# Forgetting attention: biases carried in the free rows of the second score product, causal mask added on VectorE

## The chip, the cores and the metric

The kernel runs on one core of one Trainium2 chip. The metric is the device time of one execution in microseconds; a profiled execution gives a trace besides, whose span runs from the first to the last instruction. The engines are named as in the profile: PE is TensorE (PEld its weight loads), DVE is VectorE, ACT is ScalarE, POOL is GpSimd, and SP is the engine that issues most of the DMAs.

## What is computed

One inference step of a two-layer decoder trunk for 512 prompt tokens and 8 x 4 sample tokens. Layer 0 is a state-space / sliding-window hybrid, layer 1 is forgetting attention; each is followed by cross-attention and a feed-forward block. The change is in layer 1 alone. For 16 query heads of 64 in 4 key groups it computes:

```python
q, k, v, fg = split(hp @ w_in_odd)
logf = log_sigmoid(fg + fox_fb)                       # (tokens, 16 heads)
cum  = cumsum(logf, axis=tokens)
s = einsum('qkgd,skd->kgqs', q, k) * 64**-0.5
s = s + (cum[t] - cum[s])                             # the forgetting bias
s = where(key <= query, s, -1e30)                     # causal mask
o = einsum('kgqs,skd->qkgd', softmax(s), v)           # in 128-query blocks
```

The term cum[t] is the same for all keys of a query and falls out of the softmax, so the kernel adds only -cum[s]. The sample tokens attend to 1024 cached tokens each (pages of 128 tokens, fetched by a page table) and to themselves.

## The kernel before

Activations lie transposed, features on partitions, tokens along the free dimension. A weight or activation is split into a high part that TensorE's float32r format holds and a low remainder; a linear layer is three products per 128 features (`acc3`). ACT makes the high part, DVE the low one (L158, L159 for weights).

Layer 1 is `odd`. Value and key projections come first, then the log-sigmoid, the cumulative sums, and the query projection in 8 pieces of 128 outputs (`wd_q`, two chunks of 256 and 288 tokens each, 24 products a chunk). The prompt's attention is `fox_prompt(m, c)`: m is a half of the heads (8 of 16), c a block of 128 queries, which looks at W = 128(c+1) keys. Per head it does, in order:

- four products into one PSUM bank (tag `sc`, two banks): the bias row, spread to all queries by a one-hot column (L1101, operand `oddr`); the mask of the last 128 keys in bf16 (L1102, operand `room`, 128 wide); and the scores in two products, `kh` and `kl`, W wide each (L1104). Query tiles `Q` hold the high part in 64 rows and the low part in the other 64; `kh` holds the high part of the keys in both halves of its rows, `kl` the low part in both;
- DVE: the negated maximum over the keys (L1106, TENSOR_REDUCE); ACT: the exponential from the bank into an SBUF tile `prt`, with its sum (L1110, and the read of ACT's accumulator); DVE: the reciprocal (L1111); POOL: the scaling (L1112);
- c+1 transposes on PE (L137, `room,prt`) and copies to `PT`, by DVE for even heads and ACT for odd ones (L1118).

After 8 heads the products with V follow (`PT,odd`), and DVE copies the result (L1125).

Between the heads other work is interleaved by Python generators: during m = 0 the last four query pieces (one chunk each fourth head); during m = 1 the keys and values of the cross-attention memory of the next block (`memory`, `mem_k`, `mem_v`: products `memh`/`meml` with `wxk` and `wxv` weights, "filler" below), and the sample's attention `fox_sample`, four groups G, each with S and `fox_k` products, a softmax, transposes and `fox_v` products; the table `FOX_AT` says after which heads a piece of it is written. Its pages come by SP: a group's 16 key pages and 16 value pages are issued together. The written order gives priorities only. A list scheduler with its own model of time sets the final order on each engine, and each engine then runs its list in order.

Of the kernel before, what the change touches and what calls it, by code (L numbers as in the profile page):

```python
# [9 lines left out]
F32 = mybir.dt.float32  # L10
# [9 lines left out]
P = 128  # L20
# [18 lines left out]
FOX_AT = (0, 2, 2, 3), (0, 1, 3, 5, 6), (1, 2, 6, 7), (1, 1, 5)  # L39
# [63 lines left out]
class Net:  # L103
# [880 lines left out]
    def odd(self, st, nxt, fill):  # L984
        nc, tc, I, O = self.nc, self.tc, self.I, self.O
        with ExitStack() as es:
# [35 lines left out]
            tr = ev.tile([P, 784], F32R, name="oddr")  # L1022
            ncum, self.fsel, oh16 = tr[:, 0:512], tr[:, 512:768], tr[:, 768:784]
            cw = self.H("cumw")
            strip, cum, ncx = cw[:, 0:896], cw[0:16, 896:1408], cw[0:16, 1408:1920]
            self.after(nc.scalar.dma_start(strip, I["strip"]), self.last)
            self.after(nc.vector.tensor_copy(oh16, self.cst[:, C_OH:C_OH + 16]), self.last)
            ps = self.psum("tp", [P, 512])
            for c in range(4):
                o = 384 - 128 * c  # L1030
                self.mm(ps[0:16], lf[:, c], strip[:, o:o + 512], c == 0, c == 3)
            nc.scalar.activation(cum, ps[0:16], AF.Copy, scale=-1.0)
            self.zero(ncum.bitcast(F32))
            nc.vector.tensor_copy(ncum[0:16], cum)
            nc.vector.tensor_tensor(ncx, cum, ncum[0:16].bitcast(F32), ALU.subtract)
            nc.vector.tensor_copy(ncum[32:48], ncx)
# [3 lines left out]
            with tc.tile_pool(name="fox", bufs=1) as fx:  # L1040
                self.pvs, self.heads = [], 0
                self.qst, self.prt = fx.tile([P, 3072], F32R, name="qst"), fx.tile([P, 3712], F32, name="prt")
                self.qs_at = self.pr_at = 0
                K2 = self.stack_k(kT)
# [3 lines left out]
                m0 = self.mark()  # L1048
                self.banks = ['sc']
                f = self.linear_steps(wq, range(4, 8), KD, xh, xl, qe)  # L1050
                smp = self.fox_sample(q, kTs, Qb, ncs, V, lf, fx, S, sel)
                heads = 0
                for c in range(4):
                    for _ in self.fox_prompt(q, K2, V, ncum, oh16, fx, 0, c):
                        heads += 1
                        if heads % 4 == 0:
                            next(f, None)
                        if heads == 16:
                            next(smp)
                for _ in f:  # L1060
                    pass
                self.banks = ['sc', 'sc', 'tr']
                f = fill()
                next(f)
                heads = 0
                for c in range(4):
                    for _ in self.fox_prompt(q, K2, V, ncum, oh16, fx, 1, c, FOX_AT[c], smp):
                        heads += 1
                        if heads % 4 == 0:
                            next(f, None)  # L1070
# [722 lines left out]
```

## Time and profile before

| | |
|---|---|
| median of 3 runs | 1703.76 us (1699.1 to 1706.17) |
| profiled execution | 1705.22 us, span 1703.5 us |
| mean granted clock of PE | 0.992 |
| PE busy | 1657.2 us (97%) |
| PEld busy | 1529.4 us (90%) |
| DVE busy | 1179.1 us (69%) |
| ACT busy | 772.8 us (45%) |
| POOL busy | 328.2 us (19%) |
| first and last product of the prompt's attention scores | 1012.7 and 1174.9 us from the span's start |

Busy time of PE counts matmuls by modelled ends: consecutive matmuls overlap, so the duration of one (0.27 us and more) is longer than the spacing of their starts. Where a cost of PE is asked, the spacing of starts is read. A line number in a row is that of the code before; helpers such as `mm` (L134) and `tr` (L137) carry the line of all their callers, so rows are told apart by the tiles they name.

### The profile page before, as it was taken

How to read it: one execution, taken by the hardware profiler on the slowest of the kernel's cores; microseconds unless marked ns; L12 is line 12 of the kernel's file. 1: busy time of each engine (PE TensorE's matmuls, PEld its weight loads, DVE VectorE, ACT ScalarE, POOL GpSimd, SP SyncE). 2: the span in 40 equal slices, each digit the busy share in tenths (PEclk: the TensorE clock that was granted, in tenths of full speed). 3: DMA queues.
4: the chain of work that ended last, by engine and by line, in shares of the span. 5: the costliest groups of instructions: out<-in, count | busy, mean ns of one | idle time of the engine just before them, and what ended most of it. 6: DMA issues, size and time to landing. Idle time of an engine off the chain costs nothing.

```text
span 1703.5 us, 32512 instructions
## 1 busy us (share of the span) xinstructions
PE 1657.2 (97%) x12848; PEld 1529.4 (90%) x12848; DVE 1179.1 (69%) x2212; ACT 772.8 (45%) x1599; POOL 328.2 (19%) x508
## 2 busy tenths in 40 slices
PE   7999999998999999999999999999999999999997
PEld 6988799886997999999999987666988999999997
DVE  7666678866866887677766656545577877777663
ACT  5255435344545544444445335445535354444444
POOL 5022312566412310000001203111223100000002
PEclk9999999999999999999999999999999999999999
DMA  5211424136532233222323324455551233233212
GB/s 184 64 53 42 145 79 135 47 110 238 185 111 113 87 106 112 81 99 88 106 75 134 125 66 148 132 148 194 184 189 51 75 112 100 90 103 106 75 66 87
DMA packets 71221, 189.28 MB, mean 111 GB/s; under 512 B 7612, under 2 KB 34012, under 8 KB 63452
## 3 DMA queue, kind: packets, MB, share of 16 engines
q1 hardware_dynamic: 69388, 184.84, 32.6%
q8 instruction: 101, 1.65, 0.4%
q10 hardware_dynamic: 1600, 1.83, 0.4%
q0 software_dynamic: 80, 0.52, 0.1%
q14 instruction: 52, 0.43, 0.1%
HBM read 172.22 MB, written 14.95 MB: 110 GB/s over the span
## 4 chain that ended last, share of the span: by engine, by line
PE 89%; DVE 4%; POOL 2%; DMA 2%; issue 1%; ACT 1%; DVEq 0%; ACTq 0%; POOLq 0%
PE ps L134 64%; PE ps L1512 22%; PE ps L137 3%; POOL room L421 1%; ACT split_t L158 0%; DMA lg<-fox_logf,pg 0%; DVE xs L875 0%; DVE split_t L159 0%; POOL sq L417 0%; DVE split_t L1493 0%; DMA room<-wo_e 0%; DVE xn L1450 0%; DVE meml L248 0%; DMA room<-wfi 0%; DMA o_s_ssm<-hb 0%
## 5 line engine op out<-in xcount | busy, mean ns | idle before, releaser
L134 PE MATMUL ps<-xh,split_t 128*128 128x288 f32 (+1 forms) x2304 | 466.1, 294 | 16.6 <-ACT split_t L158 12.0
L134 PEld LDWEIGHTS ps<-xh,split_t 128*128 128x128 f32 x2304 | 372.0, 191 | 23.8 <-ACT split_t L158 13.2
L1512 PE MATMUL ps<-xf,split_t 128*128 128x272 f32 x2592 | 348.9, 289 | 3.1 <-DVE split_t L1493 2.2
L134 PE MATMUL ps<-xl,split_t 128*128 128x256 f32 (+1 forms) x1152 | 338.7, 295 | 1.2 <-DVE xl L248 1.0
L1512 PEld LDWEIGHTS ps<-xf,split_t 128*128 128x128 f32 x2592 | 335.0, 188 | 4.5 <-DVE split_t L1493 3.1
L257 POOL TENSOR_TENSOR room<-room,sq 128x256 f32<-128x256 f32 (+1 forms) x96 | 86.0, 900 | 773.1 <-ACT sq L256 771.3
L134 PEld LDWEIGHTS ps<-xl,split_t 128*128 128x128 f32 x1152 | 219.2, 190 | 6.6 <-issue 4.1
L158 ACT CAST split_t<-room 128x1024 fp32r<-128x1024 f32 (+1 forms) x128 | 130.3, 1019 | 173.5 <-PE ps L134 122.6
L134 PE MATMUL ps<-hh,fs 128*128 128x256 f32 (+1 forms) x1024 | 206.3, 288 | 0.0
L159 DVE TENSOR_TENSOR split_t<-room,split_t 128x1024 fp32r<-128x1024 f32 (+1 forms) x128 | 155.7, 1219 | 30.6 <-ACT split_t L158 29.9
L134 PEld LDWEIGHTS ps<-hh,fs 128*128 128x128 f32 x1024 | 164.9, 188 | 0.4 <-ACT fs L1556 0.4
L1493 DVE TENSOR_TENSOR split_t<-fr,split_t 128x1024 fp32r<-128x1024 f32 x108 | 131.6, 1220 | 33.9 <-ACT split_t L1492 33.8
L1492 ACT CAST split_t<-fr 128x1024 fp32r<-128x1024 f32 x108 | 113.4, 1052 | 86.5 <-PE ps L1512 54.3
L134 PE MATMUL ps<-hl,fs 128*128 128x256 f32 (+1 forms) x512 | 147.3, 288 | 0.0
L134 PE MATMUL ps<-oh,split_t 128*128 128x288 f32 (+1 forms) x512 | 103.3, 294 | 1.2 <-ACT oh L242 1.2
L134 PEld LDWEIGHTS ps<-hl,fs 128*128 128x128 f32 x512 | 96.4, 188 | 0.0
L134 PEld LDWEIGHTS ps<-oh,split_t 128*128 128x128 f32 x512 | 81.7, 188 | 6.6 <-issue 4.4
L1556 ACT CAST fs<-room 128x512 fp32r<-128x512 f32 x64 | 39.4, 619 | 82.5 <-PE ps L134 67.7
L134 PE MATMUL ps<-ol,split_t 128*128 128x288 f32 (+1 forms) x256 | 76.1, 297 | 0.1
L134 PE MATMUL ps<-hh,split_t 128*128 128x256 f32 (+1 forms) x384 | 73.4, 288 | 0.0
L248 DVE SCALAR_TENSOR_TENSOR xl<-x,room,xh 128x256 fp32r<-128x256 f32 (+1 forms) x96 | 69.7, 755 | 5.3 <-ACT xh L247 5.3
L1569 DVE TENSOR_TENSOR x<-x,ps 128x256 f32<-128x256 f32 (+1 forms) x128 | 54.4, 433 | 27.0 <-PE ps L134 26.7
(417 smaller groups left out, 3132.0 us busy)
## 6 DMA issues: line engine op xcount, KB each, us to landing
fr<-wfi SPq DMA_DIRECT2D x36, 1024.0 KB
room<-wfo SPq DMA_DIRECT2D x64, 256.0 KB
room<-wo_e SPq DMA_DIRECT2D x16, 512.0 KB
xk<-mem_k SPq DMA_DIRECT2D x8, 1024.0 KB
xv<-mem_v SPq DMA_DIRECT2D x8, 1024.0 KB
room<-wfi SPq DMA_DIRECT2D x16, 512.0 KB
fox_k<-fox_k SPq DMA_DIRECT2D x64, 128.0 KB
fox_v<-fox_v SPq DMA_DIRECT2D x64, 128.0 KB
```

What stands on the lines that cost most here:

```text
L134: self.nc.tensor.matmul(out, lhsT, rhs, start=start, stop=stop)
L137: self.nc.tensor.transpose(out, in_, self.ident[0:k, 0:k])
L158: nc.scalar.copy(hi[:, 0:n], raw[:, 0:n])
L159: nc.vector.tensor_tensor(lo[:, 0:n], raw[:, 0:n], hi[:, 0:n].bitcast(F32), ALU.subtract)
L248: return nc.vector.scalar_tensor_tensor(ll, src, g, hh.bitcast(F32), ALU.mult, ALU.subtract)
L257: nc.gpsimd.tensor_tensor(acc, acc, sq[:, 0:N], ALU.add)
L421: nc.gpsimd.tensor_tensor(acc, acc, sq, ALU.add)
L1492: nc.scalar.copy(hi, t)
L1493: nc.vector.tensor_tensor(lo, t, hi.bitcast(F32), ALU.subtract)
L1512: self.nc.tensor.matmul(ps, w[a][:, k], x[:, b, k], start=start and k == 0 and i == 0, stop=k == 3 and i == 2, skip_group_check=True)
L1556: nc.scalar.copy(hi, raw)
L1569: nc.vector.tensor_tensor(x, x, ps, ALU.add)
```

## The change

The queries' low part no longer meets the keys' low part: of the second product's 128 rows, 64 are freed, and they carry the biases. Operand `Q[1]` has the high part of the queries in 64 rows and one-hot columns in the others; `kl` has the low part of the keys and, in the free rows, the cumulative sums of the group's heads (high part in 32 rows, remainder in 32). The bias product and the mask product go. The mask is a 512-wide SBUF tile of 384 zeros and 128 mask columns, added by one DVE operation that reads scores and mask, writes (score + mask) times -1 to `prt`, and keeps the minimum as the exponential's bias; ACT then reads `prt` instead of PSUM. `fox_queries` adds a DVE copy of the high part of the queries. `prt` turns through four slots instead of three. The interleaving is set by `FOX_PLAN` (head number to pieces; q = query chunk, s = sample, m = memory), the sample's first loads are written ahead of the first head, the memory's first piece comes at head 34 instead of ahead of head 33, and a group's value pages are issued after the products of the group before instead of with its key pages.

```diff
-FOX_AT = (0, 2, 2, 3), (0, 1, 3, 5, 6), (1, 2, 6, 7), (1, 1, 5)
+FOX_PLAN = {}
+for _a, _heads in (("q", range(4, 33, 4)), ("s", [33,34,36,38,40,41,43,45,47,49,51,53,55,57,59,61]), ("m", range(34, 64, 4))):
+    for _h in _heads:
+        FOX_PLAN[_h] = FOX_PLAN.get(_h, "") + _a
...
-                self.mm(ps[0:16], lf[:, c], strip[:, o:o + 512], c == 0, c == 3)
+                self.mm(ps, pad[:, c].rearrange("p g x -> p (g x)"), strip[:, o:o + 512], c == 0, c == 3)
+            cr = self.H("cumr", F32R)
+            ncum = cr[:, 0:512], cr[:, 512:1024]
+            nc.scalar.activation(ncum[0], ps, AF.Copy, scale=-1.0)
+            nc.vector.scalar_tensor_tensor(ncum[1], ps, -1.0, ncum[0].bitcast(F32), ALU.mult, ALU.subtract)
...
+    def fox_keys(self, kT, ncum):
...
+            nc.vector.tensor_tensor(kl[a, :, r], src, kh[a, :, r].bitcast(F32), ALU.subtract)
+            for m in range(2):
+                g = 32 * (2 * m + r)
+                nc.scalar.copy(kl[b:b + 32, m, r], ncum[0][g:g + 32].bitcast(F32))
+                nc.vector.tensor_copy(kl[b + 32:b + 64, m, r], ncum[1][g:g + 32].bitcast(F32))
+        for j in range(2):
+            Q = self.qst[:, 2048 + 1024 * j:3072 + 1024 * j].rearrange("p (r i t) -> p r i t", r=2, i=4)
+            for r in range(2):
+                b = 64 - 64 * r
+                d = nc.vector.tensor_copy(Q[b:b + 64, r], self.cst[0:64, C_OH:C_OH + 4].unsqueeze(2).to_broadcast([64, 4, 128]))
...
+    def fox_queries(self, q, m, tok):
...
+            nc.scalar.copy(Q[0][a, r], src)
+            nc.vector.tensor_copy(Q[1][a, r], Q[0][a, r].bitcast(F32))
+            nc.vector.tensor_tensor(Q[0][b, r], src, Q[0][a, r].bitcast(F32), ALU.subtract)
...
-                self.mm(sc[:, 0:W], oh16[:, hd:hd + 1].to_broadcast([P, P]), ncum[:, 0:W], True, False)
-                self.mm(sc[:, W - 128:W], self.identb, self.maskb[:, 128:256], False, False)
                 for z in range(2):
-                    self.mm(sc[:, 0:W], Q[:, r, i], K2[z][:, m, r, 0:W], False, z == 1)
+                    self.mm(sc[:, 0:W], Q[z][:, r, i], K2[z][:, m, r, 0:W], z == 0, z == 1)
...
-                nc.vector.tensor_reduce(nm, sc[:, 0:W], AX.X, ALU.max, negate=True)
-                nc.scalar.activation(pr[:, 0:W], sc[:, 0:W], AF.Exp, bias=nm, accum_out=den)
+                nc.vector.tensor_tensor_reduce(pr[:, 0:W], sc[:, 0:W], mask, -1.0, 1e30, ALU.add, ALU.min, nm)
+                nc.scalar.activation(pr[:, 0:W], pr[:, 0:W], AF.Exp, bias=nm, scale=-1.0, accum_out=den)
```

The programs of before and after have the same PE order up to the cumulative sums, and again from the output projection of layer 1 on; the rows between differ at three places that matter below. In the rows, `split_t` with `xh`/`xl` is the query projection's filler, `oddr` the bias, `room 128x128` the mask, `room,prt` the transposes.

PE, block c = 3 of m = 0, two heads, before:

```order
L137 MATMUL ps_11915<-room,prt 128x128 x4
L134 MATMUL ps_12008<-oddr 128x512
L134 LDWEIGHTS room
L134 MATMUL ps_12008<-room 128x128
L134 MATMUL ps_12008<-kh_10828,qst 128x512
L134 MATMUL ps_12008<-kl_10829,qst 128x512
L137 MATMUL ps_11934<-room,prt 128x128 x4
```

and PE at the same place after:

```order
L140 MATMUL ps_11900<-room,prt 128x128 x4
L137 MATMUL ps_12004<-kh_10826,qst 128x512
L137 MATMUL ps_12004<-kl_10827,qst 128x512
L140 MATMUL ps_11917<-room,prt 128x128 x4
L137 MATMUL ps_12021<-kh_10826,qst 128x512
L137 MATMUL ps_12021<-kl_10827,qst 128x512
```

The bias and mask products are gone, and the transposes that stand between two heads are those of the head four places back instead of three. PE, block c = 2 of m = 0, around its fifth head, before:

```order
L134 MATMUL ps_11791<-oddr 128x384
L134 LDWEIGHTS room
L134 MATMUL ps_11791<-room 128x128
L134 MATMUL ps_11791<-kh_10828,qst 128x384
L134 MATMUL ps_11791<-kl_10829,qst 128x384
L134 MATMUL ps_12084<-xl_10100,split_t 128x288
L134 MATMUL ps_12084<-xh_10099,split_t 128x288 x2
L134 MATMUL ps_11678<-PT_11312,odd 64x512 x3
L137 MATMUL ps_11720<-room,prt 128x128 x3
```

and PE there after, from the second head on:

```order
L137 MATMUL ps_11690<-kh_10826,qst 128x384
L137 MATMUL ps_11690<-kl_10827,qst 128x384
L140 MATMUL ps_11602<-room,prt 128x128 x2
L137 MATMUL ps_11706<-kh_10826,qst 128x384
L137 MATMUL ps_11706<-kl_10827,qst 128x384
L137 MATMUL ps_11722<-kh_10826,qst 128x384
L137 MATMUL ps_11722<-kl_10827,qst 128x384
L140 MATMUL ps_11616<-room,prt 128x128 x2
```

The query projection's products, which stood between the heads down to the eighth head of c = 2, now all stand ahead of its second head; none follows. DVE, block c = 3 of m = 0, before:

```order
L1111 RECIPROCAL ty_12015<-ty_12014 128x1
L1106 TENSOR_REDUCE ty_12032<-ps_12027 128x1
L1118 COPY PT_11901<-ps_12020 128x2x128
L1118 COPY PT_11902<-ps_12020 128x2x128
L1111 RECIPROCAL ty_12034<-ty_12033 128x1
L1106 TENSOR_REDUCE ty_12051<-ps_12046 128x1
```

and DVE there after:

```order
L1137 RECIPROCAL ty_11975<-ty_11974 128x1
L1135 ISA prt,ty_11990<-ps_11987,prt 128x512
L1135 ISA ty_11990 128x1
L1115 CAST qst<-qst 64x512
L1116 TENSOR_TENSOR qst<-q_1101_11132,qst 64x512
L1137 RECIPROCAL ty_11992<-ty_11991 128x1
L1135 ISA prt,ty_12007<-ps_12004,prt 128x512
L1135 ISA ty_12007 128x1
```

The new operation is two DVE instructions, a wide one and one of 128x1; as before, the reciprocal of one head stands ahead of the wide pass of the next.

More of the change, by code (lines that the diff above doesn't have):

```diff
@@ L1218, in fox_sample @@
             if G < 3:
-                kd = load(G + 1, kd)
+                load(keys, G + 1, "fox_k")
             yield
@@ L1248, in fox_sample @@
             self.sample_o(q, Osb, G, 1)
+            if G < 3:
+                load(vals, G + 1, "fox_v")
             yield
```

124 lines of the change are left out of this document (61 added, 63 removed).

## The prediction

> **What bounds the kernel now.** I read the chain of work that ended last first, by engine:
>
> ```profile
> PE 89%; DVE 4%; POOL 2%; DMA 2%; issue 1%; ACT 1%; DVEq 0%; ACTq 0%; POOLq 0%
> ```
>
> PE carries the end nearly everywhere, so a product taken away there is worth its time unless PE then waits. The orders agree outside the stretch from the cumulative sums to the output projection, so I read that stretch by windows (busy us, with counts, of PE, PEld, DVE, ACT, POOL; then PE's clock, DMA share, GB/s):
>
> ```profile
> 980.00:1008.00 28.00, 25.95 (x186) 23.10 (x185) 13.46 (x25) 7.85 (x8) 0.00 (x0) 0.94 0.20 59
> 1008.00:1030.00 22.00, 22.00 (x174) 20.88 (x174) 14.88 (x40) 12.76 (x33) 3.46 (x9) 1.00 0.24 73
> 1050.00:1070.00 20.00, 20.00 (x117) 13.20 (x114) 15.39 (x38) 13.03 (x37) 7.66 (x15) 1.00 0.68 210
> 1070.00:1090.00 20.00, 18.59 (x121) 11.13 (x121) 11.76 (x28) 7.66 (x20) 2.77 (x4) 1.00 0.27 80
> ```
>
> PE is full until 1070, but in 1050 to 1070 DVE is at 15.4 of 20 us: the wide blocks load DVE most. Then I read instructions in order of time. First PE, one head each of c = 3, 2, 1 and 0 (start, us, engine, line, operation):
>
> ```profile
> 1066.98 0.48 PE L134 MATMUL ps<-oddr 128*128 128x512 f32 x1
> 1067.30 0.23 PE L134 MATMUL ps<-room 128*128 128x128 bf16 x1
> 1067.34 0.47 PE L134 MATMUL ps<-kh,qst 128*128 128x512 f32 x1
> 1067.65 0.39 PE L134 MATMUL ps<-kl,qst 128*128 128x512 f32 x1
> 1067.88 0.60 PE L137 MATMUL ps<-room,prt 128*128 128x128 f32 x4
> 1068.24 0.47 PE L134 MATMUL ps<-oddr 128*128 128x512 f32 x1
> ...
> 1053.61 0.42 PE L134 MATMUL ps<-oddr 128*128 128x384 f32 x1
> 1053.87 0.23 PE L134 MATMUL ps<-room 128*128 128x128 bf16 x1
> 1053.91 0.42 PE L134 MATMUL ps<-kh,qst 128*128 128x384 f32 x1
> ...
> 1028.87 0.36 PE L134 MATMUL ps<-oddr 128*128 128x256 f32 x1
> 1029.07 0.23 PE L134 MATMUL ps<-room 128*128 128x128 bf16 x1
> 1029.11 0.36 PE L134 MATMUL ps<-kh,qst 128*128 128x256 f32 x1
> ...
> 1017.02 0.22 PE L134 MATMUL ps<-oddr 128*128 128x128 f32 x1
> 1017.08 0.23 PE L134 MATMUL ps<-room 128*128 128x128 bf16 x1
> 1017.12 0.30 PE L134 MATMUL ps<-kh,qst 128*128 128x128 f32 x1
> ```
>
> The spacing from `oddr` to `kh` is what bias and mask cost PE: 0.36, 0.30, 0.24 and 0.10 us. Then one turn of the softmax at c = 3, and two maximum passes at c = 2:
>
> ```profile
> 1073.37 0.67 DVE L1106 TENSOR_REDUCE ty<-ps 128x1 f32<-128x512 f32 x1
> 1074.14 0.69 ACT L1110 ACTIVATE prt<-ps,ty 128x512 f32<-128x512 f32 x1 [0.24 <-DVE ty L1106]
> 1074.73 0.19 ACT L1110 ACTIVATION_READ_ACCUMULATOR prt<-ps,ty 128x1 f32 x1
> 1074.95 0.16 DVE L1111 RECIPROCAL ty<-ty 128x1 f32<-128x1 f32 x1
> 1075.03 0.67 DVE L1106 TENSOR_REDUCE ty<-ps 128x1 f32<-128x512 f32 x1
> ...
> 1053.21 0.54 DVE L1106 TENSOR_REDUCE ty<-ps 128x1 f32<-128x384 f32 x1
> 1054.72 0.54 DVE L1106 TENSOR_REDUCE ty<-ps 128x1 f32<-128x384 f32 x1
> ```
>
> This is a ring. DVE's list has the reciprocal of a head ahead of the next maximum, the reciprocal waits for ACT's exponential, and that for the maximum. A turn takes 75.03 - 73.37 = 1.66 us at c = 3 and 1.51 at c = 2, whatever PE does. PE needs only 68.24 - 66.98 = 1.26 a head at c = 3. So PE is the bound only while other products stand between the heads.
>
> **The change, part by part.**
>
> *Bias and mask products.* 16 heads of each width: 16 x (0.36 + 0.30 + 0.24 + 0.10) = 16.0 us of PE, half in each m. [...]
>
> *The DVE pass.* Prices (by lines: count, then busy us, mean ns):
>
> ```profile
> L1106 DVE TENSOR_REDUCE ty<-ps 128x1 f32<-128x512 f32 x16 | 10.8, 675 | 1.9 <-PE ps L134 1.9
> L1159 DVE TENSOR_TENSOR LTS<-ps,late 128x512 f32<-128x512 f32 x2 | 1.4, 688 | 0.1
> L1152 DVE TENSOR_TENSOR late<-late,tot 128x1 f32<-128x1 f32 x7 | 1.1, 160 | 0.2
> L1034 DVE CAST oddr<-cumw 16x512 fp32r<-16x512 f32 x1 | 0.4, 415 | 2.5 <-ACT cumw L1032 2.5
> L476 DVE TENSOR_TENSOR qst<-q,qst 64x512 fp32r<-64x512 f32 x16 | 11.3, 707 | 1.8 <-ACT qst L475 1.4
> L1118 DVE COPY PT<-ps 128x256 f32<-128x256 f32 x32 | 12.7, 419 | 6.3 <-PE ps L137 5.8
> L1125 DVE COPY q<-ps 128x512 f32<-128x512 f32 x8 | 5.5, 692 | 11.1 <-PE ps L134 10.9
> ```
>
> The new operation itself is in no row. Its wide half I take at 0.69 us for 512, as L1159, which reads PSUM and a second operand and writes SBUF. Its 128x1 half lies between nothing and the 0.16 of L1152; I take 0.16, the nearest in kind. [...] So each turn of the ring grows by 0.01 + 0.16: 1.83 us at c = 3, 1.68 at c = 2. ACT's exponential reads SBUF instead of PSUM; I leave it at 0.69. The bank is free after DVE's pass instead of after ACT's, some 0.9 us earlier; PE's weight loads waited for that 4.8 us in all, which is the most it could return:
>
> ```profile
> PEld ps L134 <- ACT prt L1110: 4.8, 10, 1.0
> ```
>
> I count it inside the sums below, not on top.
>
> *The query copy.* 16 x 0.415 = 6.6 us of DVE. With its subtraction it is 1.12 us where it stands between a head's wide pass and its reciprocal. Between those DVE has idle 74.95 - 74.04 = 0.91 us (much the same at c = 2), so 0.2 sticks out each time.
>
> *First half (m = 0).* c = 0, 1 and the first head of c = 2 have filler, so PE's saving counts: 8 x (0.10 + 0.24) + 0.30 = 3.0 us. The query products that stood behind the second head of c = 2 (38 by the order) now stand ahead of it. One costs 0.136 us by the chain's row (start, us, count), so +5.2; the second row is the maximum of that head before:
>
> ```profile
> 997.55 20.96 PE ps L134 x154
> ...
> 1044.36 0.56 DVE L1106 TENSOR_REDUCE ty<-ps 128x1 f32<-128x384 f32 x1 [0.41 <-PE ps L134]
> ```
>
> After, it begins at 1044.4 - 3.0 + 5.2 = 1046.6 by that clock. From there come 14 turns without filler: 7 x 1.68 + 7 x 1.83 = 24.6, and the places where DVE's own work is longer than its gap: three query pairs 0.6, and two copies of products with V (0.69) that meet one or two `PT` copies (0.42 each at most) in a gap of 0.9, about 1.1. The last wide pass of the half begins at 1046.6 + 26.3 = 1072.9; the last maximum before, at 1075.03. Of 8.0 us released 2.1 stay: DVE's ring takes PE's place, and PE waits for banks in a stretch where it was full.
>
> *Second half (m = 1).* The order puts the memory's products down to the end of c = 1, where PE is the bound with DVE at 11.8 of 20. Then 8 heads of c = 2 and 6 of c = 3 stand without it; the output projection covers the last two. The ring for 14: 8 x 1.68 + 6 x 1.83 = 24.4, with the sample's own DVE work about 27. But PE has the sample's products there:
>
> ```profile
> L134 PE MATMUL ps<-fox_v,prt 128*32 128x128 f32 x256 | 8.8, 275 | 0.0
> L134 PE MATMUL ps<-fox_k,odd 128*32 128x512 f32 x64 | 12.8, 603 | 0.0
> ```
>
> Two of four groups, at most half of these, 10.8 us, beside the heads' own, at most 14 x 0.90 = 12.6, and the products with V: PE and ring are level, and two level lists in fixed order wait for each other a little. I charge 2 us: 6 of 8 stay. Bounds: 0 (as in the first half) and 8.
>
> *Preparation.* DVE loses two 64x1024 remainders and the 16-row copies and gains one-hot and bias copies; ACT gains four 32x512 copies. In 980 to 1008 DVE is busy 13.5 and ACT 7.9 of 28, which hides them. Where the cover is thin is the one evacuation that PE already waits for; the 0.4 to 1.2 us of a copy more ahead of it is the price if it fails, and I take zero:
>
> ```profile
> PE ps L134 <- DVE q L452: 1.8, 1, 1.8
> ```
>
> *DMAs.* On SP's queue the first page loads move ahead of three memory weights, and later value pages behind them; a queue entry that waits for a weight buffer would hold the pages behind it. The value pages are used only after that group's softmax and transposes, and the DMA share above is 0.2 to 0.7, so I take zero; one late set of 16 pages would cost what PE then lacks, a few us.
>
> *Sum.* 2.1 + 6 = 8.1 us less: 1705.2 - 8.1 = 1697.1 for the profiled execution (span 1703.5 and 1.7 around it). That execution lies 1.5 above the median of the runs, so on the median 1703.8 - 8.1 = 1695.7.
>
> **Rivals.**
>
> *A: all of PE's saving stays.* If the early release of the banks and the fourth slot of `prt` let PE run on while DVE turns, the ring hides behind filler as at c = 0 and 1: 16.0 us less, 1687.8, and with part of the 4.8 us of bank waits down to 1684. For it: PE was at 20.00 of 20 in 1050 to 1070. Against it: the reciprocal still stands between two wide passes, and two banks let PE be only two heads ahead.
>
> *B: nothing stays.* If the second half loses its saving as the first does, 0 to 4 us remain: 1700 to 1704. For it: 14 of its 32 heads have no filler. Against it: the sample's products.
>
> *C, the other side: the DVE pass runs at half speed.* The place is the ring. 512 elements cost 0.675 us and 128 fewer cost less by 0.135, so an element is about 1.05 ns; at two passes of the array a 512-wide pass takes 0.54 us longer and a 384-wide one 0.40. Over 14 uncovered heads in each half that is 2 x (7 x 0.40 + 7 x 0.54) = 13 us, 5 more than the sum saves: 1709, and up to 1715 if the 32 narrow heads (16 x 0.27 + 16 x 0.13 = 6.4) come out too. It decides for slower than before from 0.29 us more a head (8.1 / 28). Against it: L1159, of two operands, runs at 0.69. [...]
>
> **How the numbers follow.** A measurement of this kernel can tell about 0.5% from no change, 8.5 us: below 1695.2 is faster, above 1712.3 slower. The forecast has 0.47, with a range of its own from 1691 (the second half keeps all and the 128x1 half is free: 14 x 0.16 = 2.2) to 1700; half of it is on each side of the bound, a little more within. A has 0.23, B 0.17, C 0.13, half of it beyond the bound. Faster: 0.22 + 0.23 = 0.45; slower: 0.06; the same: 0.49. The range from 1686 to 1707 leaves out C and the lower end of A, less than 2 in 10.
>
> **What would show it.** In the profile after: spacing from `kh` to the next head's `kh` at c = 3 of m = 0 of about 1.8 us, where PE alone would need 0.9; the wide DVE operation at 0.69 us for 512 and its second half at up to 0.16; PE's busy share below full in the stretch that replaces 1050 to 1070, with waits of the score products for DVE; no such waits at c = 0 and 1; the start of the output projection about 8 us earlier. The prediction is wrong if the wide operation is much dearer than 0.7 (C), if PE stays full down to the end of m = 0 (A), or if the memory's products or the pages come late, which nothing above prices beyond a few us.

## The result, and the profile after

The changed kernel is slower: 1715.09 us (median of 4 runs, 1713.53 to 1716.31) against 1702.96 for the kernel before in the same set, a ratio of 1.0072 with a 95% interval of 1.0049 to 1.0095. The forecast was 1695.7, within 1686 to 1707. The profiled execution took 1713.53 us, its span is 1711.7, and PE's mean granted clock 0.984 (before 0.992). That execution was the fastest of its four and the profiled one of before lay above its median, so the spans differ by 8.2 us where the medians differ by 12.1.

The two programs differ from the cumulative sums to the output projection of layer 1, so I cut that stretch at three places that both have: the first product of the cumulative sums, the first score product `kh`, the S product of the sample's first group, and the last product of the output projection. The three pieces are called preparation, first half and second half below; up to two narrow heads of m = 1 stand ahead of that S product and so in the first half. Windows of the kernel before (columns as in the prediction: length, then busy us of PE, PEld, DVE, ACT, POOL, then PE's clock, DMA share, GB/s):

```profile
979.19:1012.66 33.47, 31.42 (x224) 27.97 (x224) 17.86 (x33) 11.38 (x13) 0.49 (x2) 0.95 0.23 68
1012.66:1074.32 61.66, 60.60 (x409) 47.99 (x407) 41.09 (x110) 36.04 (x103) 17.61 (x36) 1.00 0.43 129
1074.32:1233.60 159.28, 154.73 (x1247) 115.70 (x1247) 86.14 (x220) 75.59 (x197) 29.41 (x47) 1.00 0.52 167
```

and of the kernel after:

```profile
979.25:1015.82 36.57, 33.08 (x221) 30.87 (x220) 19.71 (x36) 17.74 (x21) 0.75 (x2) 0.86 0.24 71
1015.82:1073.55 57.73, 53.61 (x341) 41.07 (x339) 44.46 (x147) 32.98 (x93) 18.30 (x35) 1.00 0.45 138
1073.55:1241.90 168.35, 155.33 (x1189) 112.57 (x1190) 89.71 (x260) 82.29 (x207) 30.80 (x49) 0.96 0.49 158
```

From each row come three numbers. Idle is the length less PE's busy time. The half clock's price is length x (1 - clock). Work at full clock is PE's busy time less that price. After less before:

| us | length | work at full clock | PE idle | half clock |
|---|---|---|---|---|
| preparation | +3.1 | -1.8 | +1.4 | +3.4 |
| first half | -3.9 | -7.0 | +3.1 | 0 |
| second half | +9.1 | -6.1 | +8.5 | +6.7 |
| all | +8.2 | -14.9 | +13.0 | +10.2 |

The three columns add up to the length by their definition (the clock is rounded to 0.01, so the second half's price is good to 0.8 us). The 8.2 us is also the difference of the spans, so outside the three pieces nothing changed. In the two halves, where the heads are, work fell by 13.1 us of the 16.0 forecast. The saving became idle time, and then the granted clock fell to half in places, in stretches of 3.4 or 10.2 us: 3.4 us in the stretch before, 23.8 after. PE was idle for some of those stretches, which the price counts all the same; with the time that PE was busy in them, 21.0 us after and 3.4 before, the clock's price is an estimated 8.8 us instead of 10.2. Without it the kernel would have come out about level with the one before. The forecast did not price it at all.

Work is not a count of products alone. The sample's key products (`fox_k`) fill 32 columns each, and in the kernel after two, four or eight of them that start close together took 1.04 to 1.07 us of PE at full clock. Three places of it, and the sum of all 64 before and after:

```profile
1094.82 1.04 PE L137 MATMUL ps<-fox_k,odd 128*32 128x512 f32 x2
1131.00 1.05 PE L137 MATMUL ps<-fox_k,odd 128*32 128x512 f32 x4
1073.98 1.07 PE L137 MATMUL ps<-fox_k,odd 128*32 128x512 f32 x8
...
L134 PE MATMUL ps<-fox_k,odd 128*32 128x512 f32 x64 | 12.8, 603 | 0.0
L137 PE MATMUL ps<-fox_k,odd 128*32 128x512 f32 x64 | 16.6, 631 | 1.2 <-DMA fox_k<-fox_k 1.2
```

The changed order runs them in smaller groups, which costs 3.8 us of PE (about 1 of them by the half clock) and hides part of the heads' saving in the second half.

The new DVE operation itself is no dearer than forecast. By lines (count, then busy us, mean ns), wide pass and query copy:

```profile
L1135 DVE CUSTOM_DVE_ANT_0 prt<-ps,prt 128x512 f32<-128x512 f32 x16 | 10.8, 676 | 2.1 <-PE ps L137 1.6 <-PE ps L140 0.5
L1115 DVE CAST qst<-qst 64x512 fp32r<-64x512 f32 x16 | 7.1, 445 | 1.7 <-ACT qst L1114 1.5
```

676 ns is what the old maximum took (675). DVE and ACT at c = 3 of m = 0 in order of time:

```profile
1065.10 0.67 DVE L1135 CUSTOM_DVE_ANT_0 prt<-ps,prt 128x512 f32<-128x512 f32 x1
1065.69 0.08 DVE L1135 DVE_READ_ACCUMULATOR2_ANT ty<- 128x1 f32 x1
1066.66 0.16 DVE L1137 RECIPROCAL ty<-ty 128x1 f32<-128x1 f32 x1 [0.88 <-ACT prt L1136]
1066.78 0.69 DVE L1135 CUSTOM_DVE_ANT_0 prt<-ps,prt 128x512 f32<-128x512 f32 x1
...
1068.73 0.67 DVE L1135 CUSTOM_DVE_ANT_0 prt<-ps,prt 128x512 f32<-128x512 f32 x1
```

The ring turns in 1066.78 - 1065.10 = 1.68 us, and in 1.95 where copies stand in it; the seven turns of this block take 1.86 on average. Its shortest three take 1.64 to 1.68, as long as the shortest took before (1.65 to 1.68), so the 0.17 us that the forecast added to each turn is not there. The second instruction takes 0.08, not 0.16, and starts before the wide pass has ended (1065.69 against 1065.10 + 0.67). The score products wait for the ring here, as forecast; at c = 0 and 1 of m = 0 they do not:

```profile
1062.16 0.50 PE L137 MATMUL ps<-kh,qst 128*128 128x512 f32 x1 [0.68 <-DVE ty L1135]
1063.80 0.50 PE L137 MATMUL ps<-kh,qst 128*128 128x512 f32 x1 [0.58 <-DVE ty L1135]
```

In the preparation PE has a wait that the kernel before did not have, and ACT's list shows why. PE and ACT after:

```profile
994.17 7.19 PE L137 MATMUL ps<-room,LTS 128*128 128x1 f32 x32 [3.49 <-ACT LTS L1169]
...
982.89 0.60 ACT L1038 ACTIVATE cumr<-ps 128x512 fp32r<-128x512 f32 x1 [7.83 <-PE ps L137]
983.38 1.03 ACT L1087 CAST kh<-kT 64x1024 fp32r<-64x1024 f32 x1
...
988.71 2.50 ACT L1092 CAST kl<-cumr 32x512 fp32r<-32x512 f32 x4
```

and ACT before:

```profile
982.84 0.59 ACT L1032 ACTIVATE cumw<-ps 16x512 f32<-16x512 f32 x1 [3.77 <-PE ps L134]
985.91 2.03 ACT L1143 COPY LTS<-ps 128x512 f32<-128x512 f32 x2 [1.26 <-PE ps L137]
```

After, the evacuation `cumr` stands ahead of four key casts, ACT idles 7.83 us for it, and then casts and bias copies run ahead of the copies `LTS`, for which PE's next products wait. What follows on PE's clock, in windows:

```profile
989.57:992.98 3.41, 1.12 (x16) 0.98 (x16) 1.04 (x2) 3.36 (x5) 0.00 (x0) 1.00 0.54 151
992.98:994.17 1.19, 0.00 (x0) 0.00 (x0) 0.56 (x1) 1.14 (x2) 0.00 (x0) 0.52 0.02 7
994.17:1003.20 9.03, 9.03 (x42) 9.03 (x43) 3.77 (x14) 0.95 (x1) 0.00 (x0) 0.50 0.20 61
...
994.00:998.00 4.00, 3.83 (x18) 3.83 (x19) 0.18 (x2) 0.12 (x1) 0.00 (x0) 0.50 0.44 131
998.00:1002.00 4.00, 4.00 (x20) 4.00 (x20) 2.39 (x9) 0.00 (x0) 0.00 (x0) 0.50 0.01 2
1002.00:1006.00 4.00, 4.00 (x30) 4.00 (x29) 3.93 (x7) 2.09 (x2) 0.00 (x0) 0.84 0.01 4
...
1112.00:1116.00 4.00, 2.42 (x19) 1.50 (x17) 1.05 (x5) 0.27 (x1) 0.00 (x0) 0.99 0.86 290
1116.00:1120.00 4.00, 3.72 (x15) 1.87 (x16) 1.65 (x6) 2.04 (x7) 0.00 (x0) 0.50 0.08 28
```

PE's wait of 3.49 us begins at 990.68, and the clock falls at 993.0, 2.3 us into it. It then stays at half for 9.0 us in which PE is busy throughout. After 1.6 us of idle time, in pieces, in 1112 to 1116 it falls as well.

### The profile page after: what moved, and what is told of

It is laid out like the page before. It is cut to its first block, busy times and chain, and to the rows that moved or that the text cites. A ratio compares the mean times of both kernels' runs of the same rounds, so it can differ in the third digit from the quotient of the medians.

```text
span 1711.7 us, 32340 instructions
## 1 busy us (share of the span) xinstructions
PE 1652.0 (97%) x12720; PEld 1522.6 (89%) x12720; DVE 1184.8 (69%) x2296; ACT 779.2 (46%) x1603; POOL 332.1 (19%) x510
## 3 DMA queue, kind: packets, MB, share of 16 engines
q8 instruction: 100, 1.64, 0.4%
q10 hardware_dynamic: 1600, 1.83, 0.4%
```

## The experiments

Each run's three pieces come from windows like those above. "At full clock" is the second half's length less its half-clock price; both figures are good to 0.8 us. The kernel before, run beside them, had 1703.28 (e1 to e4), 1701.99 (e5 to e8), 1703.70 (e9 to e12), 1705.05 (e13 to e16) and 1702.62 (e17, e18), so across these sets the ratios or the pieces are compared rather than the medians.

| run | median us | ratio to before [95%] | preparation | first half | second half | its idle | its half clock | at full clock |
|---|---|---|---|---|---|---|---|---|
| before | 1702.96 | 1 | 33.5 | 61.7 | 159.3 | 4.6 | 0 | 159.3 |
| after | 1715.09 | 1.0072 [1.0049, 1.0095] | 36.6 | 57.7 | 168.4 | 13.0 | 6.7 | 161.6 |
| e1_prep | 1707.21 | 1.0021 [1.0005, 1.0037] | 31.4 | 57.7 | 166.7 | 10.2 | 8.3 | 158.4 |
| e2_arith | 1706.33 | 1.0022 [1.0005, 1.0038] | 35.4 | 55.6 | 163.7 | 12.8 | 3.3 | 160.4 |
| e3_plan | 1709.26 | 1.0034 [1.0020, 1.0048] | 31.7 | 62.2 | 165.5 | 12.4 | 0 | 165.5 |
| e4_loads | 1708.13 | 1.0028 [1.0011, 1.0045] | 36.5 | 57.4 | 164.1 | 10.0 | 6.6 | 157.5 |
| e5_prep_oldplan | 1702.33 | 1.0007 [0.9991, 1.0022] | 31.4 | 55.7 | 163.6 | 12.6 | 3.3 | 160.3 |
| e6_prep_loads | 1704.19 | 1.0014 [1.0004, 1.0025] | 31.4 | 57.3 | 164.7 | 12.1 | 6.6 | 158.1 |
| e7_ring | 1691.15 | 0.9937 [0.9920, 0.9953] | 29.9 | 51.9 | 159.6 | 8.4 | 1.6 | 158.0 |
| e8_pages | 1701.99 | 0.9996 [0.9985, 1.0008] | 33.0 | 57.7 | 162.9 | 14.7 | 4.9 | 158.0 |
| e9_ring_before | 1705.17 | 1.0014 [1.0002, 1.0026] | 33.2 | 59.1 | 166.6 | 10.0 | 5.0 | 161.6 |
| e10_ring_after | 1724.51 | 1.0122 [1.0100, 1.0144] | 37.9 | 53.9 | 167.6 | 13.8 | 8.4 | 159.2 |
| e11_dummy | 1696.99 | 0.9962 [0.9947, 0.9976] | 31.4 | 57.2 | 158.0 | 5.3 | 0 | 158.0 |
| e12_ring_dummy | 1695.78 | 0.9959 [0.9945, 0.9973] | 29.9 | 51.9 | 165.6 | 9.7 | 3.3 | 162.3 |
| e13_order_dummy | 1704.50 | 0.9995 [0.9984, 1.0007] | 31.4 | 55.6 | 162.7 | 12.6 | 1.6 | 161.1 |
| e14_order_before | 1711.81 | 1.0040 [1.0026, 1.0053] | 31.4 | (69.6) | (156.7) | (14.3) | (1.6) | - |
| e15_warm | 1713.22 | 1.0045 [1.0030, 1.0061] | 35.6 | 57.7 | 168.3 | 12.6 | 6.7 | 161.6 |
| e16_ring_order | 1697.09 | 0.9946 [0.9930, 0.9962] | 33.0 | 51.9 | 161.4 | 10.0 | 3.2 | 158.2 |
| e17_all_orders | 1699.18 | 0.9980 [0.9968, 0.9992] | 31.4 | 57.2 | 160.0 | 9.4 | 1.6 | 158.4 |
| e18_ring_all | 1698.37 | 0.9979 [0.9968, 0.9990] | 33.0 | 53.4 | 164.7 | 12.0 | 3.3 | 161.4 |

In e14 the first S product stands behind products of the second half, so its cut lies elsewhere.

### The parts of the change

e1_prep: the key casts are written ahead of the cumulative sums, and ACT's bias copies are ordered behind the `LTS` copies.

```diff
+            K2 = self.fox_keys(kT)            # ahead of the cumulative sums
...
-                K2 = self.fox_keys(kT, ncum)
                 S, sel = self.fox_bias(fx, klast)
+                self.fox_free(K2[1], ncum)    # the bias copies, each after the last LTS copy
```

> The changed kernel, with the four casts of the keys written ahead of the cumulative sums, and ACT's four copies of the biases ordered behind its two copies of the sample's cached sums (L1169); nothing else is moved by hand. Theory O (head of the line: in the changed kernel ACT's list stands at the evacuation of the cumulative sums with the key casts behind it, so the copies that PE waits for come 6 us later, PE idles 3.5 us, and its clock then drops to half for about 10 us): the 3.5 us wait goes, the half-clock stretch after it shrinks to what before had (3.4 us), the first score product begins 3 to 4 us earlier, and the time is 3 us under the changed kernel, 1711 to 1712. Theory D (the new DVE pass and its copies cost the time wherever they stand): no change, 1715.

It went further than expected, 7.9 us, and beyond the preparation alone: PE's wait fell from 3.49 to 0.78 us, the half-clock stretch behind it from 10.2 to 3.4 us, the preparation from 36.6 to 31.4. So the preparation's loss is shown: a list, not the work in it.

e2_arith, e3_plan and e4_loads part the arithmetic from the interleaving (`FOX_PLAN`) and the page loads.

```diff
 e2_arith: changed kernel with FOX_AT and joint loads of before
+FOX_AT = (0, 2, 2, 3), (0, 1, 3, 5, 6), (1, 2, 6, 7), (1, 1, 5)
+                kd = load(G + 1, kd)          # keys and values together
 e3_plan: kernel before with FOX_PLAN and split loads
 e4_loads: changed kernel with joint loads alone
-                load(keys, G + 1, "fox_k")
...
-                load(vals, G + 1, "fox_v")
+                kd = load(G + 1, kd)
```

> The changed arithmetic (biases in the free rows, mask on DVE, 4 slots) with the interleaving and the page loads of before: two loops, FOX_AT, the memory's first piece ahead of head 33, key and value pages issued together. Theory P (the second half lost 9 us because the new plan and the split loads bring the pages late and leave PE without filler, with the half clock that follows): the preparation keeps its 3 us loss, the first half its gain of 4, the second half gains 3 to 6: 1697 to 1700, under before. Theory D: as the changed kernel, 1712 to 1716.

> The arithmetic of before with the new plan (FOX_PLAN, one loop) and the split page loads. Theory P: the second half loses as in the changed kernel: 5 to 10 us over before, 1708 to 1713. Theory D: as before, 1703, within 3 us.

> The changed kernel with key and value pages of a group issued together as before; plan and arithmetic unchanged. If the late pages are what the second half lost: 4 to 8 us under the changed kernel, 1707 to 1711, and no half-clock stretch in the second half. If the plan (where the filler stands) is: within 3 us of it, 1712 to 1718, the half-clock stretches still there.

e2 missed: its first half is 6.0 us shorter than before's, but its preparation 2.0 and its second half 4.4 us longer. e3 hit: interleaving and split loads alone cost 6 us, and the second half is 6.2 us longer. Its idle time grew by 7.8 us; 3.0 of them are two waits of PE for pages, and the rest is spread over short waits:

```profile
1122.90 1.05 PE L137 MATMUL ps<-fox_k,odd 128*32 128x512 f32 x4 [1.88 <-DMA fox_k<-fox_k]
1126.23 1.05 PE L137 MATMUL ps<-fox_k,odd 128*32 128x512 f32 x4 [1.10 <-DMA fox_k<-fox_k]
```

e4's time hit, but its half-clock stretches stayed, so not as expected; its second half is 4.3 us shorter than the changed kernel's, 3 of them idle time.

```diff
 e5_prep_oldplan: e2_arith + the edit of e1_prep
 e6_prep_loads: e4_loads + the edit of e1_prep
```

> The changed arithmetic with the interleaving and the page loads of before, and with ACT's key casts ahead of the cumulative sums and its bias copies behind the LTS copies. Theory (the losses add up): e2_arith was 1706.3 at a first score product at 1014.8; the mended preparation brought that product to 1008.6 in e1_prep, and a half-clock stretch of 6.8 us shrank to 3.4: 4 to 7 us off 1706.3, so 1699 to 1702, with the gain still there at the output projection. Rival (the second half runs at the pace of the softmax turns and of the sample's chain, and swallows an earlier start as it did in e1_prep): the sum S of the first sample group comes at about 1064 us, but the last score product stays at 1173 to 1176, and the time at 1704 to 1707.

> The changed kernel whole, with the mended preparation of e1_prep and the joint page loads of e4_loads. Theory (the losses add up): 1715.1 - 7.9 - 7.0 = 1700.2, within 1698 to 1703. Rival (both mends cover the same wait of the second half): no better than the better of the two alone, 1705 to 1708.

e5 came 4.0 us below e2 by the medians and 2.6 by the ratios, so at the edge of what was expected or below it, and equals the kernel before. e6 came 3.9 below e4 where adding up would have given 7.9: between theory and rival. Neither keeps any of PE's saving at the end.

### The ring

In e7_ring the reciprocal, scaling, transposes and copies of a head are written behind the wide pass of the next.

```diff
-                nc.vector.reciprocal(rec, den)
-                nc.gpsimd.tensor_scalar(pr[:, 0:W], ...)
...
+                t = nc.vector.tensor_tensor_reduce(pr[:, 0:W], sc[:, 0:W], mask, ...)
+                if pend:
+                    self.fox_tail(*pend, t)   # reciprocal of the head before, ordered after t
+                pend = pr, den, PT, c, r, i
```

> As e5_prep_oldplan, but the reciprocal, scaling, transposes and copies of a head are written behind DVE's wide pass of the next head, so that the reciprocal no longer stands between two wide passes. Theory (the ring of pass, exponential and reciprocal paces the wide heads): at c = 3 a head then costs DVE 0.68 + 0.08 + 0.16 and half a copy, about 1.2 us instead of 1.8; over the 14 or so heads of each half that have no other product beside them 0.4 to 0.6 us each, 5 to 8 us a half, less where PE becomes the bound: 4 to 10 us under e5_prep_oldplan. Rival (PE or the sample's chain sets the pace and the ring hides): within 2 us of e5_prep_oldplan.

1691.15, 11.2 us under e5 and 0.63% under the kernel before: of all versions here the fastest, and a little more than expected. DVE at c = 3 in e7:

```profile
1046.70 0.69 DVE L1153 CUSTOM_DVE_ANT_0 prt<-ps,prt 128x512 f32<-128x512 f32 x1
...
1047.84 0.15 DVE L1171 RECIPROCAL ty<-ty 128x1 f32<-128x1 f32 x1
1047.91 0.67 DVE L1153 CUSTOM_DVE_ANT_0 prt<-ps,prt 128x512 f32<-128x512 f32 x1
```

This turn is 1.21 us, as expected, but it is one of the short ones: the seven of this block take 1.59 on average, against 1.86 in e5. The first half fell from 55.7 to 51.9, its idle time from 4.4 to 1.0 us, so PE is the bound there again; the second half fell by 4.0. In the profiled executions another 6.2 us lie ahead of the cumulative sums, where the lists of the two kernels are the same; those are not the edit's. The edit moves scaling, transposes and copies along with the reciprocal; which of them opened the ring was not tested.

e9_ring_before and e10_ring_after are the same edit on the kernel before and on the changed kernel.

> The kernel before with one edit: the reciprocal, scaling, transposes and copies of a head are written behind DVE's maximum pass of the next head. Theory (the ring is a limit of its own, and the old arithmetic, which needs 1.26 us of PE for a head at c = 3 against 0.90, was closer to PE's limit and so lost less to it): it gains, but less than the 11 us that the same edit gave the new arithmetic, 3 to 7 us, so 1695 to 1699. Rival (the edit gains the same whatever the arithmetic): 1690 to 1692, no dearer than e7_ring, and the change of arithmetic is then worth nothing.

> The changed kernel with that one edit alone: preparation, plan and page loads stay as changed. Theory (the ring took the saving of the second half, the preparation is a loss of its own): 1715 less the 11 us of e7_ring is 1704, within 1701 to 1707, with PE's wait for the LTS copies and the half clock behind it unchanged. Rival (the plan and the loads are what the second half waits for): 1710 or more.

Neither came as the theory had it. e9's first half gained 2.5 us, and its second half, whose lists came out otherwise, lost 7.3. In e10 the lists differ from the changed kernel's from the first products of the program on, and 6.5 us are lost ahead of the cumulative sums; so its 1724.5, though on the rival's side, is no test of the edit. In its first half the gain is there again: 57.7 to 53.9.

e16_ring_order makes the edit in the first half alone, with PE's list of the second half held to that of e13_order_dummy (below).

```diff
+                if m:                         # second half: no delay
+                    self.fox_tail(*pend, t)
+                    pend = None
```

> As e13_order_dummy, with the reciprocal of a head behind the next wide pass in the first half alone. Theory (the ring costs the first half what it cost e5 against e7, where the first half took 55.7 and 51.9 us): 3.8 us less than e13_order_dummy, 1688 to 1690. Rival (an earlier first half is swallowed by the second, as in e1_prep): the same as e13_order_dummy within 1 us.

It gained 7.4 us on e13 by the medians: 3.7 in the first half, as expected, and 1.3 in the second. The spans of the two profiled executions differ by 2.5 only, since 1.6 us were lost in the preparation and 0.9 ahead of it, where the lists of the two are the same. The absolute figure missed with that of e13. So the ring in the first half is shown in four kernels (e7, e9, e10, e16), worth 2.5 to 3.9 us there.

### The second half

e8_pages leaves the page loads of groups 1 to 3 out.

```diff
-                load(keys, G + 1, "fox_k")
...
-                load(vals, G + 1, "fox_v")
```

> As e1_prep, but the pages of group 0 serve all four groups, so that three quarters of the page loads are left out and the sample's attention of groups 1 to 3 is computed from other pages than the reference's. Theory (the page loads of a group, issued one by one by SP behind the products of the group before, set when the next group can start, and with it the second half): the last score product comes 4 us or more earlier than in e1_prep (1175.6), and the time is 1700 to 1703. Rival (loads are hidden and the softmax turns and the written order set the second half): 1705 to 1708, as e1_prep.

The last score product came 5.0 us earlier (1170.6), and the time hit, but not for the reason given: at full clock the second half is 158.0 us, and 158.4 in e1. Both kernels have the same 1190 products of PE there. In e8 the key products run in larger groups (10.6 us instead of 17.7 for the 64), and PE's work is 4.9 us less than in e1; its idle time is 4.5 us more, 14.7, spent waiting for DVE and ACT.

e11_dummy and e12_ring_dummy give PE 32 products more.

```diff
+                if m:
+                    self.mm(sc[:, 0:W], Q[0][:, r, i], K2[0][:, m, r, 0:W], True, True)
```

> As e5_prep_oldplan, with one more score product ahead of the two in each of the 32 heads of the second half; its result is overwritten. By the spacing of such a product in the profile before (0.32, 0.26, 0.20 and 0.06 us for the four widths) it is 8 x 0.84 = 6.7 us of PE. Theory (in the second half PE waits for the ring, so PE time given or taken there hardly counts): 1702 to 1705, at most 3 us more than e5_prep_oldplan. Rival (PE is the bound there): 1708 to 1710.

> As e7_ring, with the same additional product in the heads of the second half. Theory (with the ring out of the way PE is the bound again): 5 to 8 us more than e7_ring, 1696 to 1699. Rival (PE still has slack there): within 3 us of e7_ring, 1690 to 1694.

With more work e11 is 5.3 us *faster* than e5 (7.7 by the ratios), outside both expectations: in the second half work +5, idle -7.3, half clock -3.3. On e7 the same products cost 4.6 us (3.7 by the ratios), under the theory's 5 to 8; there the second half at full clock is 4.3 us longer. The additional products also move the lists, so the next runs hold those.

```diff
+                at = [x for a, n in PE_ORDER for x in range(a, a + n)]
+                for a, b in zip(at, at[1:]):
+                    self.after(self.log[b], self.log[a])
```

> As e5_prep_oldplan, with PE's order in the attention held to the one that e11_dummy had, without its additional products. From the sum of the score S of the first sample group to the end of the output projection, e5 had 147.7 us of products at full clock, 12.6 us of PE idle and 3.3 us lost to the half clock; e11 had 152.8, 5.3 and 0. Theory (the order of PE's list makes the idle time): idle stays near 5 us and the clock full, and 5 us of products go: 1692 to 1694. Rival (the additional products filled waits and kept the clock up): idle comes back to 10 us or more, with half-clock stretches, and the time is 1697 to 1702.

> As e5_prep_oldplan, with PE's order in the second half held to that of the kernel before, less the bias and mask products. Theory (the new order of the second half, not the new arithmetic, costs the saving): idle of PE falls from 12.6 us to that of before, 4.6, with no half clock: 1702.3 - 8 - 3.3 = 1691, within 1689 to 1695. Rival (the turns of the softmax and of the sample's chain have their length whatever the order, so what PE saves becomes idle): idle of 10 to 14 us and 1699 to 1704.

e13: with PE's list of e11 and without its products the idle time is back at 12.6 us, now at other waits, as the rival had it; the time, 1704.5, lies above both expectations, and the ratio is e5's within the intervals. e14: the order of before makes it worse than either expectation, with waits for POOL and four for pages, the longest 2.97 us. My theory that PE's order makes the idle time falls. In e17_all_orders the lists of DVE, ACT and POOL are held to those of e11 as well.

> As e13_order_dummy, but the lists of PE, DVE, ACT and POOL in the attention are all held to those of e11_dummy; only the 32 additional products are left out. Theory (the lists of all engines together make the idle time; e13 held PE's alone and waited 3.0 us for DVE's sPTn and 2.7 us for ACT's sO): idle of the second half stays near e11's 5.3 us and its work falls by the 5 us of the products: 1691 to 1693. Rival (the second half has a length of its own of 158 to 161 us at full clock, whatever PE carries, and PE time taken from it becomes idle): idle of 9 to 11 us, 158 us or more, and 1696 to 1700.

The rival's figures came: 32 products less, and the second half is 2.0 us *longer* than e11's; 158.4 us against 158.0 at full clock. The largest wait in e17 and the same place in e11:

```profile
1143.27 1.42 PE L136 MATMUL ps<-fox_k,odd 128*32 128x512 f32 x4 [3.02 <-DMA fox_k<-fox_k]
...
1143.86 1.05 PE L134 MATMUL ps<-fox_k,odd 128*32 128x512 f32 x4
```

In e17 the S product ahead of them runs 3.2 us earlier (1138.85, in e11 1142.05), but the products that need the pages start only 0.6 us earlier: here the pages take what PE gained. Behind this place the pair is not clean. Only the attention's lists are held, and the output projection's work is not: in e17 three of its weight casts stand on ACT at 1148, 1154 and 1157 us, in e11 at 1162, 1163 and 1170, and its first product is 4.6 us earlier.

e18_ring_all is e17's second half with e16's first.

> As e17_all_orders for the second half, with the reciprocal of a head behind the next wide pass in the first half, as in e16_ring_order. Theory (a gain of the first half reaches the end): 3 to 5 us under e17_all_orders, and under before by 8 us or more. Rival (it is swallowed by the second half): within 1.5 us of e17_all_orders.

Again the rival: the first half gained 3.8 us (1.7 of them a half-clock stretch that e17 has there) and the second gave back 4.7.

### The clock

e15_warm fills PE's wait in the changed kernel's preparation.

```diff
+        warm = self.psum("tp", [P, 512])
+        for _ in range(8):
+            self.after(self.nc.tensor.matmul(warm, self.ident, strip, start=True, stop=True), tr)
```

> The changed kernel with 8 more products (512 columns, 0.45 us each by the row of the cumulative sums) between the transposes of the page sums and the products that wait 3.5 us for ACT's LTS copies; their results are not used, so PE is busy in that wait. Theory (the half clock comes from PE's idle time, here the 3.5 us): the half-clock stretch of 10.2 us after it goes, 5 us less from the cumulative sums to the first score product, 31.5 instead of 36.6, and 1709 to 1711 in all, the second half being as it was. Rival (the half clock there has another cause): the stretch stays, 36 us and 1714 to 1716.

```profile
991.35 7.13 PE L1173 MATMUL ps<-cumw,room 128*128 128x512 f32 x16
998.32 3.73 PE L137 MATMUL ps<-room,LTS 128*128 128x1 f32 x32
```

The clock stays at 1.00 through the preparation, and the products behind the wait take 3.73 us instead of 7.19: PE's idle time is the cause of that half-clock stretch. The gain is small since I mis-sized the filling: a 512-wide product of this kind stands in the trace as two, so 8 take 7.1 us, twice what the wait needed. 3.5 of idle and 5.1 of half clock went, 7.7 of work came: 35.6 instead of 36.6. On the whole time 1.9 us went by the medians and 0.27% by the ratios, whose intervals overlap, and 1713.2 lies above the expected 1709 to 1711: the clock is shown in the trace, a gain in the time is not.

## Why the prediction was wrong, step by step

*Bias and mask products, 16.0 us:* right in size. Work at full clock fell by 13.1 us in the two halves, although the key products took up to 3.8 more.

*The DVE pass:* right for the pass itself, 0.676 where 0.69 was taken, and rival C falls: its half speed was a supposition, and no run shows it (0.543 us for 384 columns, 0.676 for 512). The 0.17 us a turn was too dear: the bare turn did not grow. That the average of 1.86 lies near the forecast's 1.83 is luck, since it has copies in it that the forecast counted apart.

*First half keeps 2.1 of 8:* right in mechanism, and small by 1.8: it kept 3.9. The last wide pass began 58.6 us after the first score product, instead of 62.4 before and a forecast 60.2. The ring took PE's place where the filler ends, and e7, e9, e10 and e16 gained there when it was opened.

*Second half keeps 6 of 8:* this failed most. It kept nothing and lost 9.1. I took PE as the bound down to the end of c = 1, priced PE's work against the ring for 14 heads behind it, and charged 2 us for lists that wait for each other. From S to the last score product of c = 1, and from there to the last one of c = 3, before and then after:

```profile
1074.32:1126.50 52.18, 50.79 (x387) 33.88 (x387) 26.91 (x82) 20.72 (x64) 7.01 (x16) 1.00 0.44 130
1126.50:1174.92 48.42, 47.06 (x432) 29.07 (x431) 26.85 (x77) 25.40 (x72) 7.97 (x15) 1.00 0.68 210
...
1073.55:1136.60 63.05, 58.87 (x386) 37.49 (x387) 32.73 (x107) 27.37 (x75) 9.29 (x19) 0.92 0.45 137
1136.60:1180.74 44.14, 38.12 (x320) 22.32 (x319) 26.55 (x89) 24.56 (x67) 7.28 (x12) 0.96 0.64 199
```

Both steps failed: where PE was to be the bound, idle time rose from 1.4 to 4.2 us and 5.0 us of half clock came, and behind it idle time rose from 1.4 to 6.0 us with 1.8 of half clock, against the 2 us charged. The wider cause is shown in part only. In 18 of the 19 kernels with the common cut the table's last column lies between 157.5 and 162.3 us, while PE's work in it runs from 143.4 to 154.7; e3, with late pages, has 165.5. What PE is given less there mostly becomes idle time, at whatever wait is next. e8 against e1 shows it with the same products, e17 against e11 with the same lists as far as the page wait; e12 against e7 does not follow it. Rival B, nothing stays, described this half; its time, 1700 to 1704, is that of e5.

*Preparation at zero:* failed; it cost 3.1 us, and 5.2 against what e1 shows it can be. I argued from busy shares (DVE 13.5 and ACT 7.9 of 28 hide the copies), and named the place where the cover was thin, but did not read ACT's list: one instruction at its head waited 7.8 us, and everything behind it came late.

*DMAs at zero:* failed with the new interleaving; e3 waits 1.9 and 1.1 us for pages, and e4, with the old loads, is 7.0 us better than the changed kernel by the medians, 4.3 of them seen in the second half.

*The clock:* no step of mine priced it. It is 10.2 us of the account (8.8 by the time that PE was busy in it), more than the whole result. In the preparation half clock came with a wait of 3.49 us, and e15, without that idle time, stays at 1.00; the clock fell 2.3 us into the wait, behind 3.41 us of which PE was busy for 1.12, and came back only after 9.0 us of busy time, 7.19 of them in the 32 products that had waited. In the second half no wait is as long. The longest waits of PE's products there (us in total, times, longest):

```profile
PE ps L137 <- DVE ty L1135: 5.1, 6, 1.4
```

No single one is over 1.4 us, and the clock still fell, behind pieces of idle time that sum to 1.6 us of 4. From 930 to 1250 us the clock of each trace changes only on a grid of 3.41 us steps, so I counted PE's idle time in every step at full clock, in all 20 traces:

| idle time in a step of 3.41 us | steps | followed by half clock |
|---|---|---|
| up to 0.63 us | 1619 | 0 |
| 0.63 to 1.2 us | 104 | 14 |
| 1.2 to 1.5 us | 40 | 6 |
| 1.5 to 1.82 us | 12 | 10 |
| over 1.82 us | 21 | 21 |

Ten of the 14 in the second row lie in the preparation. So here the idle time of a step counts, in one piece (2.3 us of a step in the preparation) or in several (1.6 us in 1112 to 1116), and more than 1.82 us of it was enough each time. e3 idled 12.4 us in its second half and kept the full clock; its idle time was spread, and no step of it has more than 1.47 us.

*What stays open:* what sets the second half's length at full clock, 158 to 162 us. At one place it is pages (e17); without pages (e8) PE waits for DVE and ACT instead. Whether a gain of the first half reaches the end is open too: in e7 and e16 it did, in e9 and e18 the second half gave it back. And between 0.6 and 1.8 us of idle time in a step, no run shows what decides on the clock.

## What to carry to other kernels

Before PE's saving is counted, ask what else takes as long in that stretch: where PE is 97% busy and a second chain (softmax turns, page loads) is level with it, less PE work can buy idle time, and idle time then a half clock, as it did here (14.9 us less work, 13.0 us more idle time, 10.2 us of half clock). Read the order of every engine's list at the place where work is moved in, not its busy share, since one early instruction that waits holds all behind it (here 7.83 us on ACT, and then 3.49 us on PE). What stands between two turns of a ring (here a head's reciprocal and what follows it) is worth moving: it gave 2.5 to 3.9 us in the first half of every kernel that tried it, but only the whole time tells whether such a gain reaches the end.

## What the runs showed of the hardware

- The fused add, scale and minimum from PSUM cost DVE no more than the plain maximum, 676 ns (after) against 675 (before) for 512 columns, and its accumulator is read by a second instruction of 0.08 us (after), half of an arithmetic operation on 128x1 (0.16, before).
- Half-clock stretches came as 3.4 us and multiples of it (3.4, 6.8 and 10.2 in the trace of after). In the one of 10.2 us in the preparation of after PE was busy for the last 9.0 without a break, and the clock still stayed at half.
- From 930 to 1250 us of the 20 traces the clock fell behind every step of 3.41 us with more than 1.82 us of idle time in it (21 of 21), and behind none with less than 0.63 (0 of 1619).
- Products that fill 32 columns each took PE 1.04 to 1.07 us at full clock in the kernel after whether two, four or eight of them started close together; two pairs in e17, 0.46 us apart, took 0.62 and 0.60. An order that splits them cost PE time: 10.6 us for 64 in e8, 17.7 in e1.
- Adding 5 us of products to PE made a kernel 5.3 us faster by the medians (e11 against e5).
